# A DiT block in fp32: 132 added TensorE products around the norms and the mixer rows

## The chip, the cores and the metric

The kernel runs on one core of a Trainium2 chip. The metric is the device time of one execution in microseconds. Three runs of the kernel before gave a median of 1361.4 us (1358.92 to 1363.43).

## The reference

Two blocks (`DEPTH = 2`) of a diffusion transformer over 256 context rows and 256 latent rows of 1024 columns, all in float32. What matters here is the frame of a block:

```python
def rmsnorm(x, g):
    y = xf * lax.rsqrt(jnp.mean(xf * xf, axis=-1, keepdims=True) + EPS)
    return (y * g.astype(jnp.float32)).astype(x.dtype)

for l in range(DEPTH):
    with_ctx = l < DEPTH - 1
    hx = rmsnorm(x, g_pre_mix[l]) * (1.0 + ax1) + sx1
    hc = rmsnorm(ctx, g_pre_mix[l]) * (1.0 + ac1) + sc1
    yc, yx = token_mixer(hc, hx, w_in[l], ...)
    x = x + gx1 * rmsnorm(yx, g_post_mix[l])
    hx = rmsnorm(x, g_pre_ffn[l]) * (1.0 + ax2) + sx2
    x = x + gx2 * rmsnorm(swiglu(hx, w_ffn_gate[l], w_ffn_up[l], w_ffn_down[l]), g_post_ffn[l])
    if with_ctx:
        ...
```

`token_mixer` projects the normalised rows, runs three mixers (mLSTM, HGRN2, differential attention) and projects their joined rows with `w_out`. In the last block only the latent rows go on (`with_ctx` is false).

## The kernel before

The 512 rows are four tiles of 128 (0 and 1 context, 2 and 3 latent); two tiles are a half. Block 0 works on both halves (`halves = (1, 0)`, latent first), block 1 from its output projection on only on the latent half (`halves = (1,)`).

Every large product is made of three: `wload` (L279) brings 512 KB of weights, ScalarE casts them to a rounded high part `whi` (L295), VectorE subtracts for the low part `wlo` (L296), and `mm` (L300) multiplies high by high, high by low and low by high. The activations stand transposed in two tiles `hT[0]` (high) and `hT[1]` (low), 1024 columns as eight blocks of 128.

How activations get there is what the change is about. `norm_rows` (L409) squares and sums a tile of `R` on ScalarE, GpSimd makes 1/sqrt (`rstd`, L401 and L402), VectorE scales the rows into `nsc` (L413). `norm_T` (L421) then takes the eight column blocks in four steps `kp` of two: four transposes on TensorE into one PSUM bank (L430; the operand that stays in the array is the rows, the moving one the identity), ScalarE and VectorE apply scale and shift (L436, L438), ScalarE casts to `hT[0]` (L440), VectorE subtracts for `hT[1]` (L441). `post_norm` (L443) goes ahead of it: VectorE and GpSimd make a factor from the sums of squares of `Z`, and VectorE adds the scaled `Z` to `R` (L450). `y_T` (L1123) brings the mixers' rows `Y` into `hT` in the same manner, with transposes at L1128 and evacuation at L1133 and L1134. `out_first` and `out_rest` (L1155, L1168) are the output projection, its second half of contraction first; `ev_z` (L1148) writes `Z` (L1151).

The transposes' banks come from `pst` (L127), a pool `psx` of three banks that all small products share. Who uses a bank next waits until its last reader is done.

`late_norm` (L1301) is the norm of the latent half for block 1. It is prepared at the end of block 0 and called in block 1 between the first projection's products for the context tiles and those for the latent ones (L674).

`warm` (L159) issues products of the identity with itself into a bank that is not read; they stand at the start of the program only, 32 of them by the numbers in `WARM`.

The order on each engine is made by a scheduler from the written order and its own estimates; a block under `tc.high_priority` goes first. On the engine, instructions run in that order. Steps of the modulation vectors (`ada_step`, L257: one DMA of 512 KB and VectorE work at L224 and L226) are spread between the weight blocks.

Of the kernel before, what the change touches and what calls it, by code (L numbers as in the profile page):

```python
# [18 lines left out]
P = 128  # L19
# [62 lines left out]

WARM = (7, 0, 10, 0, 2, 4, 6, 3)

KPOOL = (0, 1, 0, 0, 0, 0, 0)


# [12 lines left out]
def dit_block(ctx: ExitStack, tc: tile.TileContext, x, c, ctx_in, c_ctx, w_ada, b_ada, g_pre_mix,  # L100
# [3 lines left out]
    V, S, G, PE, SY = nc.vector, nc.scalar, nc.gpsimd, nc.tensor, nc.sync  # L104
# [22 lines left out]
    def pst(shape, mm=False):  # L127
        if mm:
            return psm.tile(shape, F32, tag="mm", name=nm("mm"))
        return psx.tile(shape, F32, tag="mx", name=nm("mx"))  # L130
# [16 lines left out]
    R = [None] * 4  # L147
# [11 lines left out]
    def warm(n):  # L159

        for _ in range(n):
            PE.matmul(acc0[3][:, :P], lhsT=ident, rhs=ident, start=True, stop=True, skip_group_check=True)

    warm(WARM[0])
    with tc.high_priority(offset=AHEAD):
# [243 lines left out]
    def norm_rows(t, xn):  # L409
        ss = sm.tile([P, 1], F32, tag="ss", name=nm("ss"), bufs=4)  # L410
        S.activation(xn, R[t], AF.Square, accum_out=ss)
        rs = rstd(ss, D, 1)
        V.tensor_scalar_mul(xn, R[t], rs)  # L413
        return xn

    def norm_scr(p_, tag, bufs=1):

        a = p_.tile([P, 4, 768], F32, tag=tag, name=nm("nsc"), bufs=bufs)
        return vap(a, 0, [[D, 2], [1, D]]), vap(a, 2 * D, [[512, 2], [256, 2], [1, 256]])

    def norm_T(u, s, hf, scr, xs=None):  # L421
        r = 1 if hf == 0 else 0
        xn, hs = scr
        if xs is None:
            xs = [norm_rows(2 * hf + i, xn[:, i]) for i in range(2)]
        for kp in range(KD // 2):
            pt = pst([P, 2, 2, P])
            for kk in range(2):
                for i in range(2):
                    PE.transpose(pt[:, kk, i, :], xs[i][:, (2 * kp + kk) * P:(2 * kp + kk + 1) * P], ident)  # L430
            h = hs[:, kp % 2]
            for kk in range(2):
                k = 2 * kp + kk
                src = pt[:, kk].rearrange("p a b -> p (a b)")
                if kk == 0:
                    S.activation(h[:, kk], src, AF.Identity, bias=s(r, k), scale=u(r, k))  # L436
                else:
                    V.tensor_scalar(h[:, kk], src, u(r, k), s(r, k), ALU.mult, ALU.add)  # L438
            sl = slice(hf * 256, hf * 256 + 256)
            S.copy(hT[0][:, 2 * kp:2 * kp + 2, sl], h)  # L440
            V.tensor_sub(hT[1][:, 2 * kp:2 * kp + 2, sl], h, hT[0][:, 2 * kp:2 * kp + 2, sl])  # L441
# [142 lines left out]
    for l in range(DEPTH):  # L584
        full = l == 0
# [537 lines left out]
        def y_T(hf, kps):  # L1123
            for kp in kps:
                pt = pst([P, 2, 2, P])
                for kk in range(2):
                    for i in range(2):
                        PE.transpose(pt[:, kk, i, :], Y[2 * hf + i][:, (2 * kp + kk) * P:(2 * kp + kk + 1) * P], ident)  # L1128
                for kk in range(2):
                    k = 2 * kp + kk  # L1130
                    src = pt[:, kk].rearrange("p a b -> p (a b)")
                    dh = hT[0][:, k, hf * 256:hf * 256 + 256]
                    S.activation(dh, src, AF.Copy, scale=gcol[:, k:k + 1])  # L1133
                    V.scalar_tensor_tensor(out=hT[1][:, k, hf * 256:hf * 256 + 256], in0=src, scalar=gcol[:, k:k + 1],  # L1134
                                           in1=dh, op0=ALU.mult, op1=ALU.subtract)
# [19 lines left out]
        def out_first(hf):  # L1155

            tt_ = (2 * hf, 2 * hf + 1)
            for t in tt_:
                for j in range(2):
                    zbank[t, j] = pst([P, 2, 256], mm=True)  # L1160
            for cb in range(4):
                hi, lo = wload([w_out[l, 512:1024, cb * 256:(cb + 1) * 256]])
                for t in tt_:
                    out_mm(t, cb, hi, 4, True, True, False)
                for t in tt_:
                    out_mm(t, cb, lo, 4, False, False, False)
# [21 lines left out]
        if full:  # L1188
            gg1 = {r: gate_rows(l, 0, r, ggp) for r in (0, 1)}
            y_T(1, (2, 3))  # L1190
            lockstep(*[chain(ml_half(h, 1), ml_W(h, 0)) for h in range(ML_H)])
            out_first(1)
            y_T(1, (0, 1))
            y_T(0, (2, 3))
            lockstep(*[ml_half(h, 0) for h in range(ML_H)])
            out_rest(1)
            out_first(0)
        else:
            y_T(1, (2, 3))
            lockstep(*[ml_half(h, 1) for h in range(ML_H)])  # L1200
            out_first(1)
            gg1 = {0: gate_rows(l, 0, 0, ggp)}
# [14 lines left out]
        with tc.tile_pool(name=f"ff{l}", bufs=1, reuse_waits="tile") as ff:  # L1217
# [4 lines left out]
            u1, s1_ = mod_cols(l, 1)  # L1222
            for hf in halves:
                scr = norm_scr(ff, "nsc")
                for t in (2 * hf, 2 * hf + 1):
                    post_norm(t, Z[t], zss[t])
                norm_T(u1, s1_, hf, scr)
            Z = {t: yp.tile([P, D], F32, tag=f"Y{t}", name=nm("Z")) for t in qt}
            zss = {t: sm.tile([P, 4], F32, tag=f"zss{t}", name=nm("zss")) for t in qt}
            groups = [(0, 8), (8, 8), (16, 6)]  # L1230
            for gi, (c0, ncb) in enumerate(groups):
# [48 lines left out]
                for tt_ in ([(0, 1), (2, 3)] if last and full else [qt]):  # L1280
                    held = (2, 3) if last and not full else (3,) if last else ()
                    for cb in range(4):
                        if cb not in held:
                            gemm_tm(d_src(cb), gact, tt_, lambda tt, ps, cb=cb: ev_d(tt, ps, cb))
                    if held:
                        holds = [None]
                        if len(held) == 2:

                            wh = ff.tile([P, 4, 768], F32, tag="nsc", name=nm("wh")).bitcast(F32R)
                            holds = [[[vap(wh, 1536 * i + 1024 * j, [[256, 4 - 2 * j], [1, 256]]) for i in range(2)] for j in range(2)], None]  # L1290
                        gemm_bt([(d_src(cb), h_) for cb, h_ in zip(held, holds)], gact, tt_,
                                lambda ci, t, ps: ev_d([t], ps, held[ci]))
                    if last:
                        for t in tt_:
                            post_norm(t, Z[t], zss[t], out if l == DEPTH - 1 else None)
                        if l + 1 < DEPTH and tt_[0] == 0:
                            norm_T(u0, s0, 0, norm_scr(ff, "nsc"))
                        elif l + 1 < DEPTH:
                            scr = norm_scr(stg, "qk")
                            xs = [norm_rows(t, scr[0][:, t - 2]) for t in tt_]  # L1300
                            late_norm = lambda u=u0, s=s0, scr=scr, xs=xs: norm_T(u, s, 1, scr, xs)  # L1301
        gst.close()


# [22 lines left out]
```

## Time and profile before

| | |
|---|---|
| median of 3 runs | 1361.4 us |
| profiled execution | 1362.55 us, span 1360.8 us |
| mean granted TensorE clock | 0.984 |
| TensorE busy | 1294.5 us (95%) |
| VectorE busy | 897.5 us (66%) |
| ScalarE busy | 619.0 us (45%) |
| GpSimd busy | 198.9 us (15%) |
| HBM read | 191.47 MB, 141 GB/s over the span |

The profiled execution took 1.75 us more than the span from its first to its last instruction. The granted clock is the share of full speed that TensorE's clock had; a float32 matmul stands in the profile as two records, a transpose and a product of the rounded parts as one.

### The profile page before, as it was taken

How to read it: one execution, taken by the hardware profiler on the slowest of the kernel's cores; microseconds unless marked ns; L12 is line 12 of the kernel's file. 1: busy time of each engine (PE TensorE's matmuls, PEld its weight loads, DVE VectorE, ACT ScalarE, POOL GpSimd, SP SyncE). 2: the span in 40 equal slices, each digit the busy share in tenths (PEclk: the TensorE clock that was granted, in tenths of full speed). 3: DMA queues.
4: the chain of work that ended last, by engine and by line, in shares of the span. 5: the costliest groups of instructions: out<-in, count | busy, mean ns of one | idle time of the engine just before them, and what ended most of it. 6: DMA issues, size and time to landing. Idle time of an engine off the chain costs nothing.

```text
span 1360.8 us, 25400 instructions
## 1 busy us (share of the span) xinstructions
PE 1294.5 (95%) x10166; PEld 1159.7 (85%) x10166; DVE 897.5 (66%) x1586; ACT 619.0 (45%) x1176; POOL 198.9 (15%) x316
## 2 busy tenths in 40 slices
PE   7998999999989999999999999899999997999997
PEld 5776889788988898998899888778897997999997
DVE  4899989564688997476335348566856555555555
ACT  3436452586255652222322236546526825544443
POOL 3123102111042200001000013133111201000001
PEclk9999999999989899999999999899999999899999
DMA  9872526132244687487335335532331314456663
GB/s 284 239 217 65 174 62 194 36 114 70 94 140 156 196 257 219 140 258 245 96 94 186 93 108 141 142 93 65 101 95 50 121 47 139 124 181 181 184 184 125
DMA packets 171348, 194.20 MB, mean 143 GB/s; under 512 B 10620, under 2 KB 158502, under 8 KB 171230
## 3 DMA queue, kind: packets, MB, share of 16 engines
q1 hardware_dynamic: 169806, 188.89, 45.9%
q0 software_dynamic: 1424, 3.68, 0.9%
q8 instruction: 80, 1.31, 0.4%
q14 instruction: 38, 0.31, 0.1%
HBM read 191.47 MB, written 1.08 MB: 141 GB/s over the span
## 4 chain that ended last, share of the span: by engine, by line
PE 79%; DVE 8%; ACT 5%; POOL 3%; issue 2%; DMA 2%; SPq 0%; DVEq 0%; POOLq 0%; ACTq 0%
PE mm L300 65%; PE mx L1102 2%; DVE wlo L296 2%; PE mx L957 1%; PE mx L979 1%; ACT whi L295 1%; PE mm L1090 1%; POOL rstd L402 1%; PE mx L430 1%; PE mx L973 1%; ACT Dt L1011 1%; DMA wraw<-in_w_ffn_down_dram 1%; PE mx L855 1%; PE ada L231 1%; POOL rstd L401 1%
## 5 line engine op out<-in xcount | busy, mean ns | idle before, releaser
L295 ACT CAST whi<-wraw 128x1024 fp32r<-128x1024 f32 (+1 forms) x254 | 259.0, 1021 | 447.0 <-PE mm L300 388.1
L296 DVE TENSOR_TENSOR wlo<-wraw,whi 128x1024 fp32r<-128x1024 f32 (+1 forms) x250 | 299.5, 1199 | 199.5 <-ACT whi L295 97.0
L300 PE MATMUL mm<-hT,whi 128*128 128x256 f32 (+1 forms) x1920 | 356.9, 337 | 3.6 <-ACT hT L440 2.1
L300 PEld LDWEIGHTS mm<-hT,whi 128*128 128x128 f32 x1920 | 296.9, 192 | 42.5 <-issue 3.3
L300 PE MATMUL mm<-whi,hT 128*128 128x256 f32 (+1 forms) x1792 | 265.7, 294 | 4.5 <-ACT hT L1133 2.2
L300 PEld LDWEIGHTS mm<-whi,hT 128*128 128x128 f32 x1792 | 234.5, 193 | 22.3 <-issue 10.5
L300 PE MATMUL mm<-hT,wlo 128*128 128x256 f32 (+1 forms) x960 | 185.5, 335 | 0.0
L300 PEld LDWEIGHTS mm<-hT,wlo 128*128 128x128 f32 x960 | 150.4, 191 | 17.5 <-issue 0.4
L300 PE MATMUL mm<-wlo,hT 128*128 128x256 f32 (+1 forms) x896 | 138.8, 292 | 0.0
L300 PE MATMUL mm<-whi,GT 128*128 128x256 f32 x1032 | 134.6, 284 | 1.0 <-ACT whi L295 1.0
L300 PEld LDWEIGHTS mm<-whi,GT 128*128 128x128 f32 x1032 | 128.2, 192 | 3.7 <-issue 1.7
L300 PEld LDWEIGHTS mm<-wlo,hT 128*128 128x128 f32 x896 | 119.1, 192 | 8.4 <-issue 7.6
L226 DVE SCALAR_TENSOR_TENSOR accq<-araw,csil,accq 128x1024 f32<-128x1024 f32 x63 | 81.3, 1295 | 25.9 <-DMA araw<-in_w_ada_dram 25.5
L300 PE MATMUL mm<-wlo,GT 128*128 128x256 f32 x516 | 71.3, 283 | 0.7 <-DVE wlo L296 0.7
L300 PEld LDWEIGHTS mm<-wlo,GT 128*128 128x128 f32 x516 | 65.9, 192 | 1.3 <-DVE wlo L296 1.3
L226 DVE SCALAR_TENSOR_TENSOR acc<-araw,csil,acc 128x1024 f32<-128x1024 f32 x49 | 63.7, 1321 | 4.5 <-DMA araw<-in_w_ada_dram 4.4
L401 POOL TENSOR_SCALAR rstd<-hss 128x1 f32<-128x1 f32 (+2 forms) x44 | 17.0, 386 | 242.7 <-ACT hsq L631 159.0
L1278 POOL TENSOR_TENSOR Z<-Z,gg 128x256 f32<-128x256 f32 x18 | 15.8, 889 | 246.7 <-ACT sqz L1277 246.7
L1254 DVE TENSOR_TENSOR sg<-sg,mm 128x256 f32<-128x256 f32 (+1 forms) x48 | 24.7, 518 | 34.2 <-PE mm L300 33.5
L964 ACT ACTIVATE e<-mx,damx 128x512 f32<-128x512 f32 (+1 forms) x48 | 29.3, 617 | 24.9 <-DVE damx L961 24.9
L786 ACT COPY Ck<-Kh 128x512 f32<-128x512 f32 (+1 forms) x56 | 28.8, 524 | 25.7 <-DVE Kh L811 17.9
L957 PE MATMUL mx<-qkT,qkT 48*128 48x512 f32 (+1 forms) x96 | 34.2, 562 | 6.3 <-ACT e L964 5.5
(275 smaller groups left out, 1474.2 us busy)
## 6 DMA issues: line engine op xcount, KB each, us to landing
araw<-in_w_ada_dram SPq DMA_DIRECT2D x80, 512.0 KB
wraw<-in_w_in_dram SPq DMA_DIRECT2D x68, 512.0 KB
wraw<-in_w_ffn_gate_dram SPq DMA_DIRECT2D x48, 512.0 KB
wraw<-in_w_ffn_up_dram SPq DMA_DIRECT2D x48, 512.0 KB
wraw<-in_w_ffn_down_dram SPq DMA_DIRECT2D x44, 512.0 KB
wraw<-in_w_out_dram SPq DMA_DIRECT2D x24, 512.0 KB
aw<-in_w_ada_dram SPq DMA_DIRECT2D x16, 512.0 KB
wraw<-in_w_in_dram SPq DMA_DIRECT2D x12, 256.0 KB
```

The costliest lines, as they stand in the source:

```text
L226: V.scalar_tensor_tensor(out=a, in0=raw, scalar=csil[:, k, r:r + 1], in1=a, op0=ALU.mult, op1=ALU.add)
L231: PE.matmul(ps[32 * j:32 * j + 32, :], lhsT=esel[:, r, :], rhs=accs[j // 2][r][:, (j % 2) * 512:(j % 2 + 1) * 512], start=r == 0, stop=r = ...
L295: S.copy(hi[:, :nk, :n], raw[:, :nk, :n])
L296: (eng or V).tensor_tensor(lo[:, :nk, :n], raw[:, :nk, :n], hi[:, :nk, :n], op=ALU.subtract)
L300: PE.matmul(ps, lhsT=lhs, rhs=rhs, start=first, stop=last, skip_group_check=True)
L401: G.tensor_scalar(o[:, :width], ss, 1.0 / n, EPS, ALU.mult, ALU.add)
L786: S.copy(C[:, q0:].rearrange("p (a b i) -> p b a i", b=2, i=m), vap(K_, 2 * m * pq0, [[512 + m, 2], [2 * m, np_], [1, m]]))
L957: PE.matmul(ps[:, :nk], lhsT=qkT[0][64 * j:64 * j + DA_D, h, t * P:(t + 1) * P], rhs=qkT[1][64 * j:64 * j + DA_D, h, :nk], start=True, sto ...
L964: S.activation(e[:, j, :nk], pp[j][:, :nk], AF.Exp, bias=mx[:, 2 + j:3 + j], scale=sc, accum_out=mx[:, 4 + j:5 + j])
L1102: PE.matmul(po[:, i, d_, :], lhsT=W[d_, s_][0][:, t * P - W[d_, s_][2]:(t + 1) * P - W[d_, s_][2]], rhs=Vml[:, s_, h, :], start=n_ == 0, s ...
L1254: V.tensor_mul(sg[:, :n], sg[:, :n], ps)
L1278: (V if cb == 3 else G).tensor_tensor(zs, zs, gg[1 if t < 2 else 0][:, cb * 256:(cb + 1) * 256], op=ALU.mult)
```

## The change

`fill(n, rows)` issues `n` float32 products of 128 x 128 with the identity as the operand that stays and 128 columns of some rows as the moving one, into a bank of the small pool that nobody reads. It is called with the numbers of `FILL`, on rows that a chain has just written, so that it stands behind that step:

- in `norm_T`, on the first normalised tile ahead of the transposes (5), and with `fills == 2` on the second one behind the transposes of steps 2 and 3 (8 each);
- in the norm before the FFN of block 1, on the second half of `Z` of both tiles (14 each) and on both tiles of `R` behind `post_norm` (10 each);
- in block 0 on `Y` of the two latent tiles, ahead of and behind the transposes of `y_T(1, (0, 1))` (8 each).

`norm_T` gets `fills=True` in block 1's norm before the FFN and `fills=2` in block 0's (both halves) and in `late_norm`. The norm of the context half at the end of block 0 gets none. In all 16 + 42 + 21 + 53 = 132 products.

```diff
+FILL = (14, 10, 5, 8)
...
+    def fill(n, rows):
+
+        ps = pst([P, P])
+        for _ in range(n):
+            PE.matmul(ps, lhsT=ident, rhs=rows[:, :P], start=True, stop=True, skip_group_check=True)
...
-    def norm_T(u, s, hf, scr, xs=None):
+    def norm_T(u, s, hf, scr, xs=None, fills=0):
         r = 1 if hf == 0 else 0
         xn, hs = scr
         if xs is None:
             xs = [norm_rows(2 * hf + i, xn[:, i]) for i in range(2)]
+        if fills:
+            fill(FILL[2], xs[0])
         for kp in range(KD // 2):
             pt = pst([P, 2, 2, P])
             for kk in range(2):
                 for i in range(2):
                     PE.transpose(pt[:, kk, i, :], xs[i][:, (2 * kp + kk) * P:(2 * kp + kk + 1) * P], ident)
+            if fills == 2 and kp in (2, 3):
+                fill(FILL[3], xs[1])
...
             out_first(1)
+            fill(FILL[3], Y[2])
             y_T(1, (0, 1))
+            fill(FILL[3], Y[3])
             y_T(0, (2, 3))
...
             for hf in halves:
                 scr = norm_scr(ff, "nsc")
+                if not full:
+                    for t in (2, 3):
+                        fill(FILL[0], Z[t][:, 512:])
                 for t in (2 * hf, 2 * hf + 1):
                     post_norm(t, Z[t], zss[t])
-                norm_T(u1, s1_, hf, scr)
+                    if not full:
+                        fill(FILL[1], R[t])
+                norm_T(u1, s1_, hf, scr, fills=not full or 2)
...
-                            late_norm = lambda u=u0, s=s0, scr=scr, xs=xs: norm_T(u, s, 1, scr, xs)
+                            late_norm = lambda u=u0, s=s0, scr=scr, xs=xs: norm_T(u, s, 1, scr, xs, fills=2)
```

What it moves on TensorE is shown at three places (`nsc` are the normalised rows, `mx` the small banks, `L171` the added products; lines of the change are some 9 to 20 higher).

TensorE, norm before the FFN of block 0, first half, before:

```order
L300 MATMUL mm_5022<-wlo_5270,hT_142 128x256 x4
L430 MATMUL mx_5339<-ident,nsc_5307 128x128 [waits PE_49]
L430 MATMUL mx_5339<-ident,nsc_5307 128x128 x3
L430 MATMUL mx_5348<-ident,nsc_5307 128x128 [waits PE_49]
L430 MATMUL mx_5348<-ident,nsc_5307 128x128 x3
L430 MATMUL mx_5357<-ident,nsc_5307 128x128 [waits PE_49]
L430 MATMUL mx_5357<-ident,nsc_5307 128x128 x3
L300 MATMUL mm_5435<-hT_142,whi_5438 128x256 [waits Activation_49]
```

The same place now:

```order
L441 MATMUL mx_5363<-ident,nsc_5325 128x128 x3
L441 MATMUL mx_5372<-ident,nsc_5325 128x128 [waits PE_49]
L441 MATMUL mx_5372<-ident,nsc_5325 128x128 x3
L171 MATMUL mx_5377<-nsc_5325,ident 128x128 [waits DVE_49]
L171 MATMUL mx_5377<-nsc_5325,ident 128x128 x7
L441 MATMUL mx_5390<-ident,nsc_5325 128x128 [waits DVE_49]
L441 MATMUL mx_5390<-ident,nsc_5325 128x128 x3
L171 MATMUL mx_5395<-nsc_5325,ident 128x128 [waits PE_49]
L171 MATMUL mx_5395<-nsc_5325,ident 128x128 x7
L309 MATMUL mm_5501<-hT_142,whi_5504 128x256 [waits Activation_49]
```

Before, the first step's transposes stood further up and three steps stood here; now all four steps stand here, the two groups of 8 around the last one, and the first group waits for VectorE.

TensorE, the same norm, second half, which stands among the first products of the FFN (`mm_5581` and `mm_5582`; before `mm_5515` and `mm_5516`); now:

```order
L309 MATMUL mm_5582<-hT_142,whi_5584 128x256
L171 MATMUL mx_5460<-nsc_5408,ident 128x128 [waits DVE_49]
L171 MATMUL mx_5460<-nsc_5408,ident 128x128 x7
L441 MATMUL mx_5473<-ident,nsc_5408 128x128 [waits DVE_49]
L441 MATMUL mx_5473<-ident,nsc_5408 128x128 x3
L171 MATMUL mx_5478<-nsc_5408,ident 128x128 [waits PE_49]
L171 MATMUL mx_5478<-nsc_5408,ident 128x128 x7
L309 MATMUL mm_5582<-hT_143,whi_5584 128x256
```

and before:

```order
L300 MATMUL mm_5515<-hT_142,wlo_5553 128x256 x4
L300 MATMUL mm_5516<-hT_142,wlo_5553 128x256 x4
L430 MATMUL mx_5416<-ident,nsc_5366 128x128 [waits DVE_49]
L430 MATMUL mx_5416<-ident,nsc_5366 128x128 x3
L300 MATMUL mm_5593<-hT_142,whi_5596 128x256
```

The last four transposes have moved ahead of the FFN's last upper product and its eight lower ones, with the added groups on both sides.

TensorE, norm before the FFN of block 1, where the output projection's last products end; now:

```order
L309 MATMUL mm_12227<-wlo_12476,hT_142 128x256 x4
L171 MATMUL mx_12514<-Z_12374,ident 128x128 [waits DVE_49]
L171 MATMUL mx_12514<-Z_12374,ident 128x128 x13
L171 MATMUL mx_12529<-Z_12376,ident 128x128 [waits DVE_49,PE_49]
L171 MATMUL mx_12529<-Z_12376,ident 128x128 x13
L171 MATMUL mx_12549<-R_4253,ident 128x128 [waits DVE_49,PE_49]
L171 MATMUL mx_12549<-R_4253,ident 128x128 x9
L171 MATMUL mx_12565<-R_4255,ident 128x128 [waits DVE_49,PE_49]
L171 MATMUL mx_12565<-R_4255,ident 128x128 x9
L171 MATMUL mx_12588<-nsc_12513,ident 128x128 [waits DVE_49,PE_49]
L171 MATMUL mx_12588<-nsc_12513,ident 128x128 x4
L441 MATMUL mx_12594<-ident,nsc_12513 128x128 [waits PE_49]
```

Before, the transposes of `nsc` followed on the projection's last products with nothing between; now 53 products stand there.

## Rows read from the trace of the kernel before

**Rows 1.** The page: busy time of TensorE, and granted clock in 40 slices.

```profile
PE 1294.5 (95%) x10166; PEld 1159.7 (85%) x10166; DVE 897.5 (66%) x1586; ACT 619.0 (45%) x1176; POOL 198.9 (15%) x316
...
PEclk9999999999989899999999999899999999899999
```

**Rows 2.** Stretches: length, busy by engine, granted clock (PEclk), DMA share, GB/s.

```profile
395.14:402.73 7.59, 5.62 (x27) 5.60 (x27) 6.57 (x12) 2.87 (x7) 1.48 (x2) 0.55 0.61 195
457.42:463.99 6.57, 5.85 (x26) 5.56 (x27) 5.32 (x7) 2.52 (x4) 1.19 (x2) 0.50 0.68 220
856.24:866.38 10.14, 7.68 (x28) 7.16 (x29) 7.38 (x16) 6.04 (x10) 0.00 (x0) 0.51 0.40 115
1153.74:1163.36 9.62, 5.93 (x25) 5.08 (x26) 6.08 (x10) 6.07 (x11) 1.77 (x4) 0.50 0.14 54
```

**Rows 3.** Stretches of the first block's FFN (PE, PEld, DVE, ACT, POOL, PEclk).

```profile
464.00:476.00 12.00, 11.91 (x100) 11.59 (x100) 10.82 (x14) 9.89 (x16) 2.76 (x4) 1.00 0.54 152
476.00:560.00 84.00, 84.00 (x532) 76.49 (x531) 65.26 (x73) 32.27 (x46) 0.00 (x0) 1.00 0.67 211
```

**Rows 4.** TensorE in order of time, warm-up: start, duration, what, records.

```profile
14.23 2.50 PE L162 MATMUL mm<-ident 128*128 128x128 f32 x20
16.56 0.38 PE L491 MATMUL mx<-ident,ar 128*128 128x128 f32 x2
```

**Rows 5.** All engines in order of time, norm before block 1's FFN.

```profile
1148.61 0.69 DVE L1151 TENSOR_TENSOR Z<-mm,gg 128x512 f32<-128x512 f32 x1 [1.01 <-PE mm L300]
...
1156.92 0.87 PE L430 MATMUL mx<-ident,nsc 128*128 128x128 f32 x3 [7.87 <-DVE nsc L413]
...
1158.30 3.25 PE L430 MATMUL mx<-ident,nsc 128*128 128x128 f32 x13 [0.51 <-DVE nsc L413]
1159.24 1.21 ACT L436 ACTIVATE nsc<-mx,adaC,u 128x256 f32<-128x256 f32 x2 [2.98 <-PE mx L430]
...
1161.21 3.39 PE L300 MATMUL mm<-hT,whi 128*128 128x256 f32 x16
```

**Rows 6.** All engines in order of time, norm before block 0's FFN.

```profile
452.80 1.47 PE L430 MATMUL mx<-ident,nsc 128*128 128x128 f32 x12
...
454.03 1.19 PE L300 MATMUL mm<-hT,whi 128*128 128x256 f32 x8
...
455.81 0.98 DVE L438 TENSOR_SCALAR nsc<-mx,u,adaC 128x256 f32<-128x256 f32 x2
...
457.35 0.80 PE L300 MATMUL mm<-hT,whi 128*128 128x256 f32 x2 [2.12 <-ACT hT L440]
...
458.86 1.65 PE L300 MATMUL mm<-hT,whi 128*128 128x256 f32 x6 [0.72 <-DVE hT L441]
...
460.31 1.91 PE L300 MATMUL mm<-hT,wlo 128*128 128x256 f32 x8
...
462.01 4.14 PE L300 MATMUL mm<-hT,whi 128*128 128x256 f32 x26
...
465.99 1.12 PE L300 MATMUL mm<-hT,wlo 128*128 128x256 f32 x8
...
466.95 0.88 PE L300 MATMUL mm<-hT,whi 128*128 128x256 f32 x6
```

**Rows 7.** All engines in order of time, late norm at the head of block 1.

```profile
856.58 2.61 PE L430 MATMUL mx<-ident,nsc 128*128 128x128 f32 x11 [1.08 <-DVE nsc L413]
...
860.62 0.99 DVE L438 TENSOR_SCALAR nsc<-mx,u,adaC 128x256 f32<-128x256 f32 x2
...
862.05 3.02 PE L300 MATMUL mm<-whi,hT 128*128 128x400 f32 x8
...
866.19 1.87 PE L300 MATMUL mm<-whi,hT 128*128 128x400 f32 x8
```

**Rows 8.** TensorE in order of time, mixer rows of block 0.

```profile
394.22 0.50 PE L300 MATMUL mm<-whi,hT 128*128 128x256 f32 x2 [1.39 <-ACT hT L1133]
397.11 1.97 PE L1128 MATMUL mx<-ident,Y 128*128 128x128 f32 x8 [2.39 <-DVE Y L638]
```

## The prediction

> **What bounds the kernel now.** I read the page first: TensorE is busy 95% of the span, and the row of the granted clock is full but for a few slices near the 12th, the 13th and 14th, the 26th and the 35th [rows 1]. Those are the places of the change. The table by stretches then gives each fall its edges [rows 2]: four stretches at or next to the lower of the two levels (1.2 instead of 2.4 GHz), at 395, 457, 856 and 1154 us. The reader is to see two things there. First, the engine had little to do before each: 1153.74 lies inside a wait of 7.87 us [rows 5], and 457.42 stands right behind one of 2.12 us [rows 6]. Second, the price of the low level is bounded: busy time in the four stretches times what the clock lacks is 5.62 x 0.45 + 5.85 x 0.50 + 7.68 x 0.49 + 5.93 x 0.50 = 12.2 us. More than that no warm clock can give back.
>
> Between these places TensorE has no room: from 464 to 476 us it is busy 11.91 of 12.00 us, and from 476 to 560 all of 84 us, at full clock [rows 3]. What is added there, or runs past the end of a wait, moves the end of the kernel.
>
> I number the places by time: 1, mixer rows of block 0 (16 added products); 2 and 3, the norm before the FFN of block 0, first and second half of the tokens (21 each); 4, the late norm at the head of block 1 (21); 5, the norm before the FFN of block 1 (53). Together 132.
>
> **Price of one added product.** The warm-up products have the same shape, type and stationary operand. A warm-up group of 10 stands as 20 records and takes from 14.23 to 16.56 us until the next instruction starts [rows 4]: 2.33 us, 0.23 us for a product of two records. So the 132 cost 30.4 us of TensorE at the high clock. At the low one I take twice that (an estimate: the eight low-order products of the FFN take 1.91 us at the low clock and 1.12 at the high one [rows 6]).
>
> The Trainium skill, page "TensorE: Matmul & The Clock Gate", section "Back-to-back issue gap", gives about 81 ns for a 128-column matmul in a stream of weight loads and matmuls. By it the 132 would cost 10.7 us (an estimate from that page) and the sum below would be about -5 us instead of +7.5; the row of the warm-up speaks against it for this operand type.
>
> **Place 5.** The groups of 14, 14, 10, 10 and 5 stand one behind the other on TensorE, ahead of all transposes. The first can start when VectorE has written the second half of Z, at 1148.61 + 0.69 = 1149.30 [rows 5]; the operands of the others are ready when their turn comes. 53 x 0.23 = 12.2 us, so they end at 1161.5. Before, the main group of transposes started at 1158.30: they now start 3.2 us late. From there to the first product of the FFN took 2.91 us; the first read by ScalarE came 0.94 us after the transposes' start, and with the clock high about 0.35 us of this goes. The first product comes at 1164.05, not 1161.21: 2.85 late. The clock gives back: the first 16 products took 3.39 us, and at the high rate (8 in 0.96 us, from 465.99 to 466.95 [rows 6]) 16 x 0.12 = 1.9 and some 0.2 until the last one's end, so 1.3 us. Net **+1.5 us**; ends: +0.2, if all 2.97 us of the stretch's price come back, and +3.2, if none.
>
> **Place 3.** 21 products, 4.8 us, in a stretch in which TensorE waited 0.1 us and the clock was full [rows 3]: nothing covers them and nothing is given back. The second group of 8 now has only eight products of the FFN ahead of it while VectorE reads the first bank of transposes, so some more can be lost. **+4.8 us**; ends 3.8 and 6.
>
> **Place 2.** The group of 5 stands behind seven of the eight first products of the output projection, which themselves wait for VectorE; I take 1.0 of its 1.15 us as lost (ends 0 and 1.6: the four transposes behind it now go to the later group as well). The twelve transposes that ran from 452.80 (1.47 us [rows 6]) then run from 453.8 to 455.2. The next group of 8 waits for VectorE's read of the first bank; before, VectorE came to these reads at 455.81, 0.98 us for two; 1 us later the first is done at 457.2. Eight products 1.84, four transposes 0.5, eight products 1.84: the FFN starts at 461.4. Before, by 464.0, when the clock had come back, TensorE had done 8 + 2 + 6 + 8 products and 9 of the 26, 33 in all [rows 6]; after, 2.6 / 0.12 = 21.6. It is 11.5 products, **+1.4 us**, behind. Ends: 0 and, with the clock low through the added products, +4.8.
>
> **Place 4.** The group of 5 is covered by a wait of 1.08 us [rows 7]. The twelve transposes behind it run at the high clock. The group of 8 again waits for VectorE's read of the first bank, at 860.62 before; the shorter transposes let it come 0.5 us earlier or so, so its end is 860.6. 1.84 + 0.5 + 1.84 later, at 864.75, the projection starts, 2.7 us after 862.05. Its 12 products from there to 866.19 took 4.14 us at the low clock; half of this, 2.07, is saved. **+0.6 us**; ends -1.5 and +3.4.
>
> **Place 1.** The first group of 8 fills the wait of 1.39 us [rows 8] and part of the next. The transposes at 397.11 wait for VectorE's Y as before. From there to 402.73 TensorE was busy 5.6 us at the low level, 2.8 at the high; with 1.84 us of added products in it, 4.65. **-0.9 us**; ends -2.5 and +2.3.
>
> No other engine gets an instruction, and no DMA is added; VectorE's and ScalarE's orders change only around places 1 to 3. I cost that at nothing and keep 3 us either way for it.
>
> Sum: 1.5 + 4.8 + 1.4 + 0.6 - 0.9 = +7.4 us. The profiled execution took 1362.55 us (span 1360.8 and 1.75 around it), 1.15 above the median 1361.4; against its own time the sum gives 1370, against the median 1368.8. I predict **1369 us**, own range 1365.5 to 1372.
>
> **Rivals.**
> *The clock falls all the same.* In places 2 and 4 the first added products now stand behind twelve transposes and wait for VectorE, about 2 us and 2.5 us; in place 1 about 2.2 us stay open before 397.11. The fall at 457.42 came after a wait of 2.12 us [rows 6], so each can fall. Then the added products run at 0.46 us in front of the real ones: +3.4 in place 2, +2.8 in place 4, +3.2 in place 1. One fall gives 1372, two 1375, all three 1378.5. For it: the transposes and the wait stand together, with no products between. Against it: long runs of products now stand around these waits, and in place 4 the five products come before.
>
> *Faster: the added products are cheap.* If one takes the time of a transpose, 0.12 us (12 in 1.47 [rows 6]), the groups of place 5 end at 1155.7, ahead of the second normalised row, and cost nothing there; places 5, 3, 2, 4, 1 give -1.65, +2.5, -0.5, -1.1, -1.85: -2.6 us, 1359. The point from which it decides is a product of about 0.15 us, where the sum is nothing. For it: products of twice the columns take 0.12 us in the FFN. Against it: the warm-up, 0.23 for the same form. This is also the side on which the page's 81 ns lies (1356.5 by the sum above).
>
> *No change: later waits swallow it.* If the FFN of block 0 had slack that the busy row hides (pipelined matmuls are drawn long), the 4.8 us of place 3 would be regained before block 1: 1364. Against it: 84.00 of 84.00 us busy [rows 3] with the other engines at 78% and less.
>
> **How the numbers follow.** A measurement can tell 0.3% here, 4.1 us: faster is below 1357.3, slower above 1365.5. Forecast 0.40, a fallen clock 0.26, cheap products 0.12 (of which 0.07 faster), swallowed 0.12 (0.10 within), and 0.10 for changed orders that I did not price (0.03, 0.04, 0.03). Faster 0.10, same 0.05 + 0.10 + 0.04 = 0.19, slower 0.40 + 0.26 + 0.02 + 0.03 = 0.71. The range 1358 to 1376 takes in one and two fallen clocks and most of the cheap case; about 0.08 lies out on either side.
>
> **What would show it.** In the profile after: the added products of place 5 as one run of about 12 us, its transposes at about 1161.5 plus the shift so far; the clock full from there on; 21 added products between 464 and 480 with TensorE busy throughout; the second group of 8 in places 2 and 4 started only after VectorE's read. Wrong I am if an added product takes 0.15 us or less, or if the time from place 3 to the end of the FFN of block 0 is not longer by about 5 us.

## The result and the profile after

| | before | after |
|---|---|---|
| median of four runs | 1360.9 us | 1373.2 us |
| profiled execution (span) | 1362.55 (1360.8) us | 1374.57 (1372.8) us |
| mean granted TensorE clock | 0.984 | 0.993 |

The changed kernel is slower: its time is 1.0092 times that of before, 95% interval 1.0078 to 1.0107. That is 12.3 us, where 7.4 were forecast; 1373 lies inside the range of 1358 to 1376, but 1.2 us above the forecast's own 1365.5 to 1372.

The page of the changed kernel, TensorE and its granted clock in 40 slices, the answer to [rows 1]:

```profile
PE 1317.2 (96%) x10430; PEld 1183.7 (86%) x10430; DVE 897.4 (65%) x1586; ACT 619.4 (45%) x1176; POOL 204.4 (15%) x316
PEclk9999999999999999999999999999999999999999
```

The clock now looks full, and the kernel is slower all the same: TensorE has 264 more records and 22.7 us more busy time. The table by stretches shows what the tenths hide (length, busy by engine, granted clock behind POOL; against [rows 2]):

```profile
396.50:400.50 4.00, 3.57 (x18) 3.60 (x19) 3.62 (x6) 1.31 (x3) 0.00 (x0) 0.57 0.69 229
458.00:462.00 4.00, 4.00 (x23) 4.00 (x23) 4.00 (x10) 1.70 (x5) 2.25 (x3) 0.57 0.95 350
867.50:871.50 4.00, 3.69 (x18) 3.69 (x19) 2.54 (x5) 1.70 (x3) 0.00 (x0) 0.57 0.69 203
1058.50:1062.50 4.00, 4.00 (x18) 3.44 (x17) 2.06 (x6) 2.90 (x10) 0.58 (x2) 0.57 0.00 0
```

At places 1, 2 and 4 the clock fell again. The falls are shorter: a mean of 0.57 over 4 us is 3.4 us at the low level, where before it was 6.6 to 10. But now the added products stand in them. Only the fall of place 5 is gone; a new one, at 1058.5, lies where the change adds nothing.

TensorE in order of time at place 5, against [rows 5] (start, duration, what, records, wait ahead and who ended it):

```profile
1160.06 6.52 PE L171 MATMUL mx<-Z,ident 128*128 128x128 f32 x56 [0.31 <-DVE Z L1164]
1166.41 4.63 PE L171 MATMUL mx<-R,ident 128*128 128x128 f32 x40
1170.88 1.28 PE L171 MATMUL mx<-nsc,ident 128*128 128x128 f32 x10
1171.99 1.47 PE L441 MATMUL mx<-ident,nsc 128*128 128x128 f32 x12
```

28 products take 6.35 us from 1160.06 to 1166.41: 0.227 us each, the price that the warm-up gave. All 53 run as one stretch of 11.93 us up to the transposes. This place went as forecast.

Place 3, against [rows 3] and [rows 6]:

```profile
470.43 1.35 PE L171 MATMUL mx<-nsc,ident 128*128 128x128 f32 x10 [0.20 <-DVE nsc L422]
...
472.99 1.20 PE L309 MATMUL mm<-hT,whi 128*128 128x256 f32 x8
474.59 2.05 PE L171 MATMUL mx<-nsc,ident 128*128 128x128 f32 x16 [0.41 <-DVE nsc L451]
...
476.92 1.95 PE L171 MATMUL mx<-nsc,ident 128*128 128x128 f32 x16
```

Nothing hides these 21 products, and two waits of 0.61 us in all are new.

Place 2 and, below it, place 4, against [rows 6, 7]:

```profile
454.20 1.47 PE L441 MATMUL mx<-ident,nsc 128*128 128x128 f32 x12
457.73 3.37 PE L171 MATMUL mx<-nsc,ident 128*128 128x128 f32 x16 [2.05 <-DVE nsc L451]
460.89 0.97 PE L441 MATMUL mx<-ident,nsc 128*128 128x128 f32 x4
461.69 1.95 PE L171 MATMUL mx<-nsc,ident 128*128 128x128 f32 x16
463.39 2.16 PE L309 MATMUL mm<-hT,whi 128*128 128x256 f32 x16
...
864.15 1.61 PE L441 MATMUL mx<-ident,nsc 128*128 128x128 f32 x12
867.81 3.67 PE L171 MATMUL mx<-nsc,ident 128*128 128x128 f32 x16 [2.05 <-DVE nsc L451]
871.32 0.60 PE L441 MATMUL mx<-ident,nsc 128*128 128x128 f32 x4
871.75 1.95 PE L171 MATMUL mx<-nsc,ident 128*128 128x128 f32 x16
873.46 1.69 PE L309 MATMUL mm<-whi,hT 128*128 128x400 f32 x8
```

In both, the first group of 8 does not fill the wait for VectorE: it stands behind it, because its bank is the one that VectorE is reading. The wait of 2.05 us stays, the clock falls 0.5 us behind it at place 2 and right at its end at place 4 (granted 0.50 from 458.20 and from 867.81 us), and the group runs at the low level: 3.16 us from 457.73 to 460.89 and 3.51 from 867.81 to 871.32, where the second group takes some 1.7 at the full clock. Only then come the last four transposes, the second group and the FFN or the projection.

Place 1, against [rows 8], and a later place in the output projection:

```profile
391.97 1.95 PE L171 MATMUL mx<-Y,ident 128*128 128x128 f32 x16
...
396.93 0.45 PE L1141 MATMUL mx<-ident,Y 128*128 128x128 f32 x1 [2.57 <-DVE Y L651]
...
398.23 2.67 PE L171 MATMUL mx<-Y,ident 128*128 128x128 f32 x14
...
430.64 1.22 PE L309 MATMUL mm<-whi,hT 128*128 128x256 f32 x8 [1.55 <-ACT sqz L1166]
```

The second group partly falls into the low clock, and at 430.64 stands a wait of 1.55 us that before did not have.

**Where the time went.** VectorE subtracts the low part of each of 250 weight blocks (L296, now L305), in the same order in all kernels here. The start of the same block's subtraction, minus its start in the profile before, gives the shift at that point (the heads give the block's number, counted from 0, and its start before). Between one block ahead of a place and one behind it the shift changes by what the place cost (us, from the profiled executions):

| kernel | 37: 386.1 | 49: 448.2 | 77: 563.6 | 133: 841.1 | 149: 902.2 | 173: 1076.2 | 193: 1186.3 |
|---|---|---|---|---|---|---|---|
| place between | | 1 | 2, 3 | | 4 | | 5 |
| all (the change) | -0.3 | 1.3 | 9.0 | 7.8 | 9.2 | 10.7 | 12.3 |
| one product per group | 0.5 | 0.8 | 0.5 | -0.7 | -4.3 | -1.2 | -2.1 |
| place 5 alone | -1.6 | -1.7 | -2.8 | -3.5 | -4.8 | -3.3 | -1.6 |
| place 3 alone | 1.1 | 0.9 | 5.5 | 3.5 | 3.6 | 5.1 | 5.3 |
| place 1 alone | -0.5 | 1.3 | 1.0 | 0.5 | 1.2 | 3.7 | 4.0 |
| place 2 alone | -1.1 | -2.1 | 4.0 | 2.1 | 1.8 | 5.9 | 5.1 |
| place 4 alone | -0.8 | -1.1 | -1.9 | -3.7 | -2.1 | -2.2 | -3.0 |
| own bank | 0.1 | 0.8 | 3.1 | 2.9 | -0.4 | 1.0 | -0.4 |
| one product at 2 and 4 | -0.4 | -0.7 | -2.1 | -3.2 | -6.0 | -2.9 | -4.4 |
| places 1 and 2 | -0.8 | 0.9 | 3.8 | 1.9 | 0.8 | 0.7 | -0.2 |
| side queues, none | 0.1 | 0.1 | -0.7 | -1.6 | -3.0 | -1.7 | -2.5 |
| side queues, place 2 | -0.3 | -1.6 | 0.9 | -0.3 | 0.3 | 0.2 | 0.3 |
| combined | 0.1 | 0.3 | -0.9 | -2.7 | -5.8 | -4.3 | -5.8 |

In the change: place 1 +1.6, places 2 and 3 +7.6, the stretch up to block 133, where nothing is added, -1.2, place 4 +1.5, the mixers of block 1 +1.5, place 5 +1.6. A step where a kernel adds nothing shows how far one execution wanders: -1.4 to +0.7 at place 4, -0.9 to +0.3 at place 5, -1.1 to -0.2 at places 2 and 3, 0 to +4.1 in the mixers of block 1. So a step of 1 us says little by itself, and the medians below decide.

### The profile page after: what moved, and what is told of

It reads as the page before. It is cut to its first block, busy times and chain, and to the rows that moved or that the text cites. A ratio compares the mean times of both kernels' runs of the same rounds, so it can differ in the third digit from the quotient of the medians.

```text
span 1372.8 us, 25925 instructions
## 1 busy us (share of the span) xinstructions
PE 1317.2 (96%) x10430; PEld 1183.7 (86%) x10430; DVE 897.4 (65%) x1586; ACT 619.4 (45%) x1176; POOL 204.4 (15%) x316
## 4 chain that ended last, share of the span: by engine, by line
PE 58%; DVE 4%; ACT 3%; POOL 1%; issue 1%; DMA 1%; DVEq 0%; SPq 0%; POOLq 0%; ACTq 0%
PE mm L309 51%; PE mx L171 2%; DVE wlo L305 1%; PE mx L1115 1%; DMA wraw<-in_w_ffn_down_dram 1%; PE mx L970 1%; POOL Kh L824 0%; ACT whi L304 0%; PE mm L1103 0%; PE mx L992 0%; PE ada L240 0%; ACT nsc L420 0%; PE mx L986 0%; DMA wraw<-in_w_in_dram 0%; ACT Ck L799 0%
## 5 line engine op out<-in xcount | busy, mean ns | idle before, releaser
L305 DVE TENSOR_TENSOR wlo<-wraw,whi 128x1024 fp32r<-128x1024 f32 (+1 forms) x250 | 300.6, 1203 | 201.5 <-ACT whi L304 97.1
L309 PEld LDWEIGHTS mm<-hT,whi 128*128 128x128 f32 x1920 | 293.9, 190 | 39.6 <-issue 3.3
L410 POOL TENSOR_SCALAR rstd<-hss 128x1 f32<-128x1 f32 (+2 forms) x44 | 20.0, 454 | 243.8 <-ACT hsq L644 161.2
L411 POOL TENSOR_TENSOR rstd<-rstd,mhalf 128x1 f32<-128x1 f32 (+2 forms) x58 | 41.9, 723 | 4.7
```

Source lines behind the costliest of these rows:

```text
L305: (eng or V).tensor_tensor(lo[:, :nk, :n], raw[:, :nk, :n], hi[:, :nk, :n], op=ALU.subtract)
L309: PE.matmul(ps, lhsT=lhs, rhs=rhs, start=first, stop=last, skip_group_check=True)
L410: G.tensor_scalar(o[:, :width], ss, 1.0 / n, EPS, ALU.mult, ALU.add)
L411: G.tensor_tensor(o[:, :width], o[:, :width], mhalf[:, :width], op=ALU.pow)
```

## The experiments

All are made from the changed kernel; times are medians, each against before's on the same chip.

**One product per group.**

```diff
-FILL = (14, 10, 5, 8)
+FILL = (1, 1, 1, 1)
```

> Every group keeps its place, with one product each (17 instead of 132). Theory A (the added products cost their own time and the end of the wait that each group stands behind): 115 of 132 products go, so nearly all of the +12.3 us goes: 0 to +3 us against before, the rest being the waits for a bank that the one product still has to make. Rival B (the added calls change the order of the other work on TensorE, VectorE and ScalarE, and that costs): the order stays as in the changed kernel or near it, so +6 us or more stays.

1359.8 against 1360.8 us, ratio 0.9995 (0.9985 to 1.0004). Theory A, with no loss left at all: it comes with the number of products. But B is not dead by it: the wait at 430 is gone here too, so the order had moved back as well.

**Place 5 alone.** The other calls of `fill` are taken out.

```diff
-            fill(FILL[3], Y[2])
-            fill(FILL[3], Y[3])
...
-                norm_T(u1, s1_, hf, scr, fills=not full or 2)
+                norm_T(u1, s1_, hf, scr, fills=(0) if full else 1)
...
-late_norm = lambda u=u0, s=s0, scr=scr, xs=xs: norm_T(u, s, 1, scr, xs, fills=2)
+late_norm = lambda u=u0, s=s0, scr=scr, xs=xs: norm_T(u, s, 1, scr, xs)
```

> Added products in the norm before the FFN of block 1 alone (53). Theory A: they end 3.2 us after the point where the main transposes started before, and the clock gives 1.3 to 2.9 back: +1.5 us (+0.2 to +2). Rival B (order): nothing of the order ahead of this place changes, so the same +1.5. Rival C (the products are as good as free, the clock pays for them): 0 or less. Where it is not within +0.5 to +2.5, the profiles' +1.6 for this place was no sum of these terms.

1362.3 against 1360.8, +1.5 us, ratio 1.0010 (1.0001 to 1.0018); the step in the table is +1.6. That is A's number and also B's, which said the same here; C is out.

**Place 3 alone** (likewise; `norm_T` gets `fills=2` for the context half of block 0 only).

> Added products in the second half of the norm before the FFN of block 0 alone (21). Theory A: 21 x 0.23 us = 4.8 us and 0.6 us of waits for VectorE's reads, nothing hidden and nothing given back: +5.4 us. Rival B (what the two profiles show as +5.5 us here comes from the shift at place 2 and from the order, not from the products): +2 us or less. Rival C (later slack of the FFN swallows it): 0 to +1.

1366.7 against 1360.8, +5.9 us, ratio 1.0045 (1.0031 to 1.0059). Theory A; its rows read as in the change, with the same waits of 0.21 and 0.41 us. No later slack takes any of it back.

**Place 1 alone** (the two calls on `Y` stay).

> Added products at the mixers' rows of block 0 alone (16). Theory A as predicted (8 of 16 run in a wait, the rest is paid by a higher clock): -0.9 us. Rival B (the scheduler puts the mixers' products and the output projection in another order, a bank then waits for the squares of Z): +2 us, and the wait of about 1.5 us ahead of a group of eight products of the output projection is there again. Rival C (the clock falls all the same and the second group runs at 0.4 us a product): +1.5 to +2 us without that wait.

1365.0 against 1360.8, +4.2 us, ratio 1.0038 (1.0025 to 1.0050): the wrong sign of mine, and more than B or C said. The step at the place is +1.7. The rest of the profile's +4.0 stands behind block 149, where nothing was added; whether the median holds the same is not settled. The wait that B named is there. The last eviction of `Z` of the latent half, VectorE in order of time, before:

```profile
423.69 0.66 DVE L1151 TENSOR_TENSOR Z<-mm,gg 128x512 f32<-128x512 f32 x1
```

and with place 1 alone, with ScalarE's step behind it and the product that waits:

```profile
429.00 0.66 DVE L1164 TENSOR_TENSOR Z<-mm,gg 128x512 f32<-128x512 f32 x1
...
429.75 0.60 ACT L1166 ACTIVATE sqz<-mm 128x512 bf16<-128x512 f32 x1 [0.30 <-DVE Z L1164]
...
430.50 1.22 PE L309 MATMUL mm<-whi,hT 128*128 128x256 f32 x8 [1.53 <-ACT sqz L1166]
```

Sixteen more products made the scheduler put the mixers' small steps ahead of this eviction on VectorE, which comes 5.3 us later; the next half's projection needs the bank. No added product is near. But this wait is not what the place costs. From 428 to 447 us TensorE is busy equally long in both (stretches as above, before and then place 1 alone):

```profile
428.00:447.00 19.00, 16.03 (x110) 12.50 (x109) 16.64 (x25) 9.68 (x19) 8.62 (x15) 1.00 0.51 153
428.00:447.00 19.00, 16.03 (x108) 12.14 (x107) 15.66 (x29) 10.01 (x22) 8.33 (x15) 1.00 0.35 112
```

Before, four waits of 0.36 to 1.41 us made up the 2.97; now it is three, of 1.53, 0.80 and 0.64. So the wait has moved, not grown, and the size of the step is rather C's (+1.5 to +2).

**Place 2 alone** (`fills=2` for the latent half of block 0 only).

> Added products in the first half of the norm before the FFN of block 0 alone (21). Theory A: the group of 5 is absorbed, the two groups of 8 stand behind a wait for VectorE of about 2 us, and what they cost at the low clock the clock behind them gives back in part: +1.5 to +2.5 us. Rival C (the clock at this place falls in some executions only, whatever stands there, as the run with the added products of block 1 alone shows it full at 458 us): then nothing is given back on the average that was not there before, and the place costs its 3.7 us of products: +3 to +4.

1369.5 against 1360.3, +9.2 us, ratio 1.0065 (1.0046 to 1.0084): far outside both, though six executions leave it between 6 and 11; in the profile places 2 and 3 show +6.1. The trace has a chain over five engines (one line from each engine's order of time; first GpSimd, SP and ScalarE before, then all five with place 2 alone):

```profile
442.33 0.19 POOL L1119 TENSOR_SCALAR gcol<-cols 128x3 f32<-128x3 f32 x1 [1.66 <-DVE hT L1134]
...
447.12 0.37 SPq L292 DMA_DIRECT2D wraw<-in_w_ffn_gate_dram  x1
...
452.04 1.05 ACT L295 CAST whi<-wraw 128x1024 fp32r<-128x1024 f32 x1 [1.20 <-PE mm L300]
...
440.91 3.55 POOL L1132 TENSOR_SCALAR gcol<-cols 128x3 f32<-128x3 f32 x1 [1.66 <-DVE hT L1147]
...
449.54 0.37 SPq L301 DMA_DIRECT2D wraw<-in_w_ffn_gate_dram  x1
...
453.17 1.04 ACT L304 CAST whi<-wraw 128x1024 fp32r<-128x1024 f32 x1 [3.75 <-DMA wraw<-in_w_ffn_gate_dram]
...
456.58 0.99 DVE L451 TENSOR_SCALAR nsc<-mx,u,adaC 128x256 f32<-128x256 f32 x2
...
457.18 3.39 PE L171 MATMUL mx<-nsc,ident 128*128 128x128 f32 x16 [4.32 <-DVE nsc L451]
```

GpSimd's 128 x 3 step took 3.55 us; before it took 0.19. SP has a small load that waits for GpSimd, with the FFN's second block of weights behind it in its queue: its DMA is issued at 449.54 (before 447.12, though this kernel was 1 to 2 us ahead at the place). So ScalarE's cast, VectorE's low part and its read of the transposes are late, and the added group waits for that read: 4.32 us.

**Place 4 alone** (`fills=2` in `late_norm` only).

> Added products in the late norm at the head of block 1 alone (21). Theory A: the 5 are covered by a wait, the two groups of 8 stand behind another and are paid back in part by the clock: +0.6 to +1.5 us. Rival C: the clock falls all the same and the groups run at 0.4 us a product ahead of the projection: +3 us.

1362.1 against 1360.3, +1.9 us, ratio 1.0014 (1.0006 to 1.0023); the step is +1.6, as in the change. Between A and C.

**Groups in a bank of their own.** No products at places 1 and 3; one group of 8 instead of two at 2 and 4, behind the third step, in the bank of the modulation's products; place 5 cut to 37.

```diff
-FILL = (14, 10, 5, 8)
+FILL = (14, 2, 5, 8)
...
-    def fill(n, rows):
+    def fill(n, rows, own=False):
...
-        ps = pst([P, P])
+        ps = psa.tile([P, 512], F32, tag="ada", name=nm("ada"))[:, :P] if own else pst([P, P])
...
-            if fills == 2 and kp in (2, 3):
-                fill(FILL[3], xs[1])
+            if fills == 2 and kp == 2:
+                fill(FILL[3], xs[1], own=True)
```

> No products at places 1 and 3. At places 2 and 4 one group of 8 right behind the third step's transposes, in a bank that VectorE is not reading, so that it runs inside the wait of 2.1 us instead of behind it; 5 as before. At place 5 groups of 14, 14, 2, 2 and 5, 37 products, 8.5 us of a gap of 9.0. Theory A (what costs is only what ends behind the wait; what fills the wait is free and holds the clock): place 5 -1.5, place 2 -1.5 to -2, place 4 -1.5 to -3: -4 to -6.5 us against before. Rival B or C (the order changes, or the clock falls by chance whatever is there): between -1.5 and +1.

1362.4 against 1360.3, +2.1 us, ratio 1.0015 (1.0006 to 1.0024): outside A's range and B's, a miss, though two steps are as A said or better (place 4 -3.3, place 5 -1.4). Place 2 cost 2.4 us, and TensorE in order of time says why (the modulation's products before, then this run):

```profile
435.52 1.90 PE L231 MATMUL ada<-accq,esel 128*32 128x512 f32 x6
...
437.26 0.50 PE L309 MATMUL mm<-whi,hT 128*128 128x256 f32 x2 [2.19 <-ACT hT L1146]
...
455.67 1.95 PE L171 MATMUL ada<-nsc,ident 128*128 128x128 f32 x16
457.68 1.04 PE L240 MATMUL ada<-accq,esel 128*32 128x512 f32 x2
458.66 0.66 PE L441 MATMUL mx<-ident,nsc 128*128 128x128 f32 x4
...
459.48 1.90 PE L240 MATMUL ada<-accq,esel 128*32 128x512 f32 x6
```

The group fills the wait, but the modulation's own products (L240), which share the bank, now stand in front of and among the FFN's first: 2.9 us. Before, they ran among the waits around 437 us; without them a wait of 2.19 us stands open there. The filler has displaced real work from another wait.

**One product at places 2 and 4.** As the run before, without the new bank:

```diff
-FILL = (14, 10, 5, 8)
+FILL = (14, 2, 5, 1)
...
-            fill(FILL[2], xs[0])
+            fill(1 if fills == 2 else FILL[2], xs[0])
```

> No products at places 1 and 3, place 5 as in the run with the groups in a bank of their own (14, 14, 2, 2, 5), at places 2 and 4 one product where the change has 5, 8 and 8. Theory A: one product cuts the wait in two but fills none of it; the clock falls as before or somewhat later: -1.5 us from place 5 and 0 to -2 from the others, behind the run with groups of 8. Rival D (what holds the clock is that no single wait is long, not how many products stand there; the run with one product in each group had no fall at either place): -4 us or more, as good as the groups of 8 or better.

1357.1 against 1360.3, ratio 0.9974 (0.9964 to 0.9983): -3.2 us, faster than both kernels. Place 2, TensorE in order of time, against [rows 6]:

```profile
453.86 1.08 PE L309 MATMUL mm<-hT,whi 128*128 128x256 f32 x7
455.71 0.49 PE L171 MATMUL mx<-nsc,ident 128*128 128x128 f32 x2 [0.78 <-DVE nsc L451]
456.67 0.51 PE L309 MATMUL mm<-hT,whi 128*128 128x256 f32 x2 [0.47 <-ACT hT L453]
...
459.96 3.28 PE L309 MATMUL mm<-hT,whi 128*128 128x256 f32 x26
```

Seven products of the FFN stay ahead of the wait, which is cut into 0.78 and 0.47, and the 26 products behind it take 3.28 us instead of 4.14: full clock. The median lies in A's range (-1.5 to -3.5) and falls short of D's -4; but at place 2 the trace is D's, as in the run with one product in every group and in the combined one; in five of the six profiles without an added product here the clock fell. At place 4 it fell here and did not with one product in every group, so there D is open.

**Places 1 and 2 together.**

> Places 1 and 2 together. Theory A (place 1 makes TensorE late, and place 2 then waits for VectorE, whose read comes at nearly the same time whatever place 1 does: 457.2 us in the run with place 2 alone, 457.7 with all five): the two together cost little more than place 2 alone, +7 to +10 us. Rival E (the places add): +4.2 and +9.2, +13 us or more.

1365.3 against 1359.9, +5.4 us, ratio 1.0041 (1.0028 to 1.0055). E is out: not 13, and even less than place 2 alone, below A's +7 too. The group waits until 457.29 (2.04 us), with place 2 alone until 457.18: VectorE's read sets the time, and what place 1 loses disappears in that wait. The FFN's second weights were issued at 448.62, 0.9 us earlier than with place 2 alone: the side chain is shorter here.

**The small loads on GpSimd's queue**, without any added product, as a control,

```diff
-                SY.dma_start(out=ba[64 * i + r:64 * i + r + 33:32, :]
+                G.dma_start(out=ba[64 * i + r:64 * i + r + 33:32, :]
...
-                SY.dma_start(out=gp[r:r + 33:32, :]
+                G.dma_start(out=gp[r:r + 33:32, :]
```

> The kernel before, with the four loads of the modulation's bias and the two of the post-norm's weights of a group issued by GpSimd instead of SP. It is the control for the next run: -1 to +2 us (GpSimd issues more; SP's weight loads no longer stand behind a wait for GpSimd).

and **with place 2**:

> Place 2 alone, with those small loads issued by GpSimd. Theory F (part of what place 2 costs is no product: GpSimd is late there, SP waits for it with the FFN's weights queued behind, and so ScalarE's cast, VectorE's low part and its read of the transposes come late): against its control +4 to +6.5 us instead of +9.2, the wait ahead of the first group of 8 shorter than 4.3 us, the FFN's first weights cast before 452 us. Rival G (it is the order on TensorE alone, two groups of 8 in front of the eight products of the FFN that ran in the wait): +8 to +10 against the control, as before.

The control: 1362.6 against 1359.9, ratio 1.0021 (1.0012 to 1.0030), a little more than I had set. With place 2: 1366.6, so +4.0 against the control (some 2 us uncertain, by the two intervals) instead of +9.2. Theory F, at the edge of its range; G's +8 is out. The trace with place 2, GpSimd, ScalarE and TensorE:

```profile
441.45 3.55 POOL L1132 TENSOR_SCALAR gcol<-cols 128x3 f32<-128x3 f32 x1 [1.66 <-DVE hT L1147]
...
451.14 1.05 ACT L304 CAST whi<-wraw 128x1024 fp32r<-128x1024 f32 x1 [1.19 <-PE mm L309]
...
455.54 2.05 PE L171 MATMUL mx<-nsc,ident 128*128 128x128 f32 x16 [2.16 <-DVE nsc L451]
```

GpSimd is as late as with place 2 alone, but nobody stands behind it: the cast of the second block comes 2.0 us earlier, the wait is half as long, and the clock is full.

**Combined**: one product per group at place 2, the bank of its own at place 4 (where the modulation has no work), place 5 cut to 37.

> No products at places 1 and 3; at place 2 one product per group; at place 4 the 5 and, in a bank of their own behind the third step, 8; at place 5 14, 14, 2, 2 and 5. Theory A, from the steps that the profiles of the two runs before show by place (-1.4, -3.1 and -1.5): -5 to -6 us against before, 1.5 to 2.5 us better than one product at place 4. Rival C (what the clock gives at one place falls again behind it, as in the mixers of block 1): -3 to -4, no better than one product each.

1356.7 against 1359.9, ratio 0.9975 (0.9966 to 0.9983): -3.2 us, no better than one product at place 4, as rival C said. TensorE at place 4, before and then here:

```profile
861.31 1.09 PE L430 MATMUL mx<-ident,nsc 128*128 128x128 f32 x4 [2.12 <-DVE nsc L438]
...
855.16 1.95 PE L171 MATMUL ada<-nsc,ident 128*128 128x128 f32 x16
857.38 0.65 PE L441 MATMUL mx<-ident,nsc 128*128 128x128 f32 x4 [0.27 <-DVE nsc L453]
```

At place 4 the wait of 2.12 us is down to 0.27, and the clock is full there and at place 5 (granted 1.00 from 1144 to 1166 us). My -5 to -6 was read from steps against a single profile of before, whose time was 2.6 us above before's median on this chip; against that profile this one does show -5.8. Of the 1.4 us by which it is ahead of one product at places 2 and 4 in the table, the mixers of block 1, untouched in both, give 1.6 and place 4 only 0.3. A clean gain of place 4 over one product is not shown.

**The clock over all fourteen profiles.** At place 1 it fell in all. At place 5 it stayed full in the five with 37 or 53 products there and fell in the nine with none or one per group. At place 4 it stayed full in the two with the group in a bank of its own and in one of the two with one product per group, and fell in the other ten, all eight without a product among them. At place 2 it stayed full in the four with one product per group or the bank of its own; it fell in three of the four with groups behind the wait, and in five of the six with none.

## Why the prediction was right in sign and too small

**The price was right.** 0.23 us per product was forecast and 0.227 measured, so cheap products are out as a rival. The 81 ns that the Trainium skill gives for a matmul of 128 columns ("TensorE: Matmul & The Clock Gate", "Back-to-back issue gap") does not hold for this operand type: the trace disagrees by a factor of 2.8.

**Place 5, +1.5: right.** +1.5 by the median alone, +1.6 in both profiles, with the run of 12 us and the full clock behind it.

**Place 3, +4.8 (3.8 to 6): right in kind, a little small.** +5.9 alone by the median, +4.6 by the table. The missing part that a row shows is the two waits, 0.6 us, of which I had said only that "some more can be lost".

**Place 4, +0.6: too small.** +1.9 alone. The term that failed is the group of 8 "1.84 + 0.5 + 1.84": the first group took 3.51 us because the clock fell at the end of the wait ahead of it. That was the rival of the falling clock, but by the table it gave +1 and not +2.8; the low stretch lasted 3.4 us and not 10.

**Place 2, +1.4 (0 to 4.8): wrong.** Alone it costs 9.2 us by the median and 6.1 by the table. Two things failed. "Eight products 1.84": 3.16, low clock. And "No other engine gets an instruction ... I cost that at nothing": VectorE's and GpSimd's order of events moved, SP's queue stood, and the read that the group waits for came late; taking SP's queue out of it took about 5 us away by the medians, some 3 by the steps of the profiles. The 4.0 left fit the price of the products (16 at 0.23 are 3.7 us) with little given back; no run separates that. In the change it looked milder (places 2 and 3 together 7.6, place 3 alone 4.6 by the table). There place 1 had already made TensorE late, and GpSimd's step took 1.21 us instead of 3.55; which of the two counts more is not shown.

**Place 1, -0.9: wrong sign.** +1.6 in the profile, +4.2 by the median alone. The term that failed is the 2.8 us at the high clock from 397.11 on: the clock fell here all the same, and the second group ran partly at the low level. The changed order put a new wait of 1.5 us at 430 but took as much out of the waits behind it. Where the other 2.5 us of the median arise is open.

**The sum.** Medians of the five places alone add to about +22.5, the change is +12.3: the places share waits, so neither my sum of terms nor a sum of experiments was bound to hold. That 1373 lies in the range is in part luck. It is owed to the 3 us kept for the orders and to the rival of the fallen clock, which gave 1375 for two falls and 1378.5 for three; three fell, each for less than I had priced. And 1.5 us of the profile's 12.3 stand in the mixers of block 1, where nothing was added (see the last section). The rival of later slack is out (place 3 alone).

## What to carry to other kernels

Filler work only helps where it runs inside the wait: ask which bank, buffer or operand the filler itself waits for, and put no real work behind it that ran in the wait before. Size it from the row of the wait (37 products in a gap of 9 us gained 1.4 us by the table where 53 lost 1.6), and try one instruction before eight. Count a scheduled kernel's order, side queues included, as a cost of its own, and measure parts together as well as alone.

## What was not expected of the hardware

**The same wait does not always cost the clock.** In the mixers of block 1 stands a wait of 1.6 us in front of two products, with the same instructions around it. The stretch behind it, in the profile before and in the one with one product per group (length, busy by engine, clock):

```profile
1048.70:1053.00 4.30, 4.24 (x29) 3.48 (x30) 2.06 (x6) 3.44 (x11) 0.59 (x2) 1.00 0.01 4
```

```profile
1044.40:1049.50 5.10, 5.04 (x18) 3.83 (x19) 2.24 (x7) 3.48 (x11) 0.59 (x2) 0.56 0.00 0
```

In four of the fourteen profiles, before's among them, the clock stays full here and the step in the table is about zero; in the others it falls for 3.4 or 6.8 us and the step is +1.4 to +4.1 us. Place 5 alone likewise had the full clock at place 2 without any change there. And at 130 us, ahead of every added product, behind a wait of 2.4 us, the low stretch is 6.8 us long in three of the fourteen, 3.4 us in ten and missing in one. What decides is not settled; a single profile can't carry a claim of 1 or 2 us about the clock.

**A GpSimd step of 0.19 us can take 3.55.** While the 128 x 3 step ran from 440.91 to 444.46, VectorE went without a gap through four instructions on the modulation's rows and the weights (441.34 to 445.60); before, its read of the transposes stood among them. The step took 0.19 or 0.20 us in the nine profiles with no product or one per group at place 2, and 0.62 to 3.55 us in the five with groups of 5 and 8 there, so it goes with the changed order. The Trainium skill, "SBUF — State Buffer", section "SBUF: two separate sides", says that GpSimd and VectorE lock each other out of a shared pair of ports for whole instructions, VectorE's with two inputs in SBUF among them. The trace agrees: the step ends within 0.1 us of the end of one of these (443.20 + 1.21). No run takes VectorE's work away, so the lock itself is not shown. Nor is it clear why the step was not through in the 0.43 us before the first of the four began at 441.34: before, it needed 0.19 next to the same instruction of VectorE (the sum into `ba`).
